# Weight sums by accumulating transfers: moving half of the sums of the plain stages from VectorE to the DMA engines, and one matrix's sums entirely

## The chip, the cores and the metric

The kernel runs on one core of one Trainium2 chip. The metric is the device time of one launch in microseconds (us), the median of three runs. A core has a matrix engine (TensorE, PE in the profile, with its weight loads shown as PEld), a vector engine (VectorE, DVE), a scalar engine (ScalarE, ACT), a general engine (GpSimd, POOL) and an engine that here only issues transfers (SyncE, SP). Transfers between the large memory (DRAM) and the on-chip memory run on 16 DMA engines. A transfer is issued from the SP queue or from the POOL queue; each queue issues in order, and an issue that waits for a semaphore holds up everything behind it on that queue.

## The reference

One inference step of a two-layer decoder on 1024 prompt tokens and 8 decode tokens, all in float32, model width 2048:

```python
def pool_layer(x, prefix, pos, w_in, w_grp, scale, w_out, g_ln, b_ln):
    z = x @ w_in                                   # 2048 -> 4096: u and gate
    u, gate = z[..., :D_POOL], z[..., D_POOL:]
    d, new_state = multiscale_pool(u, prefix, pos) # causal windows 2, 4, 8, 16
    d = jnp.einsum('btgc,gce->btge', d.reshape(B, T, 4, 512), w_grp)
    d = d.reshape(B, T, D_POOL) * scale
    y = (d * jax.nn.silu(gate)) @ w_out
    return layer_norm(ALPHA * x + y, g_ln, b_ln), new_state

def attn_layer(x, pos, kb, vb, ...):               # after kv = h @ w_kv, rotary k
    z = x @ w_in                                   # 2048 -> 4096: q and gate
    o = attn_core(rope(q), kb, vb, ..., sinks)     # window 128, 4 KV heads, 32 heads
    y = (o * jax.nn.silu(gate)) @ w_out
    return layer_norm(ALPHA * x + y, g_ln, b_ln)
```

The outputs are the two results, the new pooling states and the new key and value windows.

## The kernel before

**Stages.** The tokens are cut into two chunks: chunk 0 has 512 prompt tokens, chunk 1 has 512 prompt tokens and the 8 decode tokens. Eight stages follow one another: `ai0`, `ai1` (input product of layer A for chunk 0 and 1, pooling, group product), `ao0`, `ao1` (its output product), `bi0`, `bi1` (key/value, query and gate products of layer B, and the attention), `bo0`, `bo1` (its output product and the last LayerNorm). By the lines that run, `ai0` lasts from 0 to about 410 us, `ai1` to 765, `ao0` and `ao1` to 1110, `bi0` to 1585, `bi1` to about 2030, and the `bo` stages to the end.

**Products.** Every float32 product is made of three fast products: an operand is split into a rounded part ("hi", cast on ACT, line 359) and a remainder ("lo", subtraction on DVE, line 368), and PE multiplies hi by hi, hi by lo and lo by hi. A weight matrix comes in pairs of output tiles; a pair has four blocks of 128 x 1024 numbers (512 KB): a11 and a12 from one tile, a21 and a22 from the other.

- The *plain* stages `ai0` and `bi0` multiply the four blocks as they are (`unit`, lines 529 to 554). One block takes 24 matmuls of 512 columns.
- The other six stages use a seven-product scheme of the Strassen kind (`seven`, lines 439 to 527): three blocks as they are and four sums of blocks. One of the seven takes 24 matmuls of 256 or 260 columns.

**The sums of weights** have to be in DRAM (the tensors `ws`, shown as swia, swoa, swkv, swib, swob in the profile) before a seven-product stage reads them:

- s2 = a21 + a22 (slot 1 of `ws`), s1 = a11 + a21 (slot 2), s3 = a11 + s2 (slot 0), s4 = a12 + s3 (slot 3).
- For `wia`, `wkv` and `wib` they are made beside the plain stage that loads these blocks anyway: `plain_pair` (line 256) puts four calls of `add1` (line 247) on the list `late`, and `end` (line 389) runs one of them per step. `add1` is one addition of 128x1024 on DVE (line 249) and one store issued from POOL (line 250).
- For `woa` and `wob`, which no plain stage reads, `sum_gen` (line 325) does it as side work: 16 parts for each matrix, each with four loads of 256 KB issued from SP (line 334), four additions of 128x512 on DVE (line 342) and four stores of 256 KB issued from POOL (line 343). `woa`'s are put on the side list in `ai0` and must be done before the inputs of `ao0` are begun; ten of `wob`'s parts are put on it in `ai1` and six in `bi0`, and all must be done before the inputs of `bo0` are begun.

**The order of the work** is written out by the program. `begin` (line 380) loads weight blocks five ahead of the one that PE is to multiply (seven, or six, in the seven-product stages), casts four ahead and makes lo three ahead. `end` closes a step: it runs what was put there by `at(n, ...)` ("n steps from now") and, every second or third step, one turn of the first generator on the side list, if enough of the 53 buffers are free. A plain block has two steps of 12 matmuls, a pair therefore eight; one of the seven products is one step of 24 matmuls. Both kinds of step hold about the same PE time. Each engine runs its instructions in the order of the source. In the plain stages POOL also clears small regions that DVE or ACT then fill (line 798 in the pooling, line 1375 in the attention), and in all stages it issues the stores of intermediate results (lines 654, 885, 1014, 1053, 1449).

In `bi1`, after each pair of query tiles, four transfers issued from SP (line 1217) swap partitions; three steps later DVE does the rotary products on what they brought (lines 1225 and 1332), and one step after that PE computes scores from it (line 1360).

## Time and profile before

| quantity | value |
|---|---|
| median of three runs | 2408.71 us (2408.36 to 2408.85) |
| the profiled execution, its own time | 2407.74 us |
| its span, first to last instruction | 2406.0 us |
| DMA queue fed by SP | 482.16 MB, 60.3% of the 16 engines' span |
| DMA queue fed by POOL | 160.88 MB, 16.9% |

The profiled execution was 0.97 us shorter than the median of the runs. A row of grouped instructions gives the line, the engine, the operation, the tile written and the tile read with their shapes, how often it ran, its busy time and the mean of one. A row of a window gives the window, the busy time of each engine with the number of its instructions in brackets, the granted clock of PE (1.00 is full), the mean share of the 16 DMA engines' time that was busy, and the GB/s moved. A DMA's landing time runs from its issue to the last byte. Since matmuls overlap, a busy PE is not proof that it runs at its best rate; the number of matmuls in a window shows that.

### The profile page before, as it was taken

How to read it: one execution, taken by the hardware profiler on the slowest of the kernel's cores; microseconds unless marked ns; L12 is line 12 of the kernel's file. 1: busy time of each engine (PE TensorE's matmuls, PEld its weight loads, DVE VectorE, ACT ScalarE, POOL GpSimd, SP SyncE). 2: the span in 40 equal slices, each digit the busy share in tenths (PEclk: the TensorE clock that was granted, in tenths of full speed). 3: DMA queues.
4: the chain of work that ended last, by engine and by line, in shares of the span. 5: the costliest groups of instructions: out<-in, count | busy, mean ns of one | idle time of the engine just before them, and what ended most of it. 6: DMA issues, size and time to landing. Idle time of an engine off the chain costs nothing.

```text
span 2406.0 us, 43031 instructions
## 1 busy us (share of the span) xinstructions
PE 2368.2 (98%) x16956; PEld 2174.7 (90%) x16956; DVE 1788.4 (74%) x2173; ACT 1244.2 (52%) x2271; POOL 216.2 (9%) x425
## 2 busy tenths in 40 slices
PE   8999999999999999999999999999999999999996
PEld 6888888999999999998878888899999999999996
DVE  8676687767768768867797676786666667788877
ACT  4222224544545546644464445564666667646655
POOL 1121211101010000000011121100000000000000
PEclk9999999999999999999999999999999999999998
DMA  9887888887889879988588766586556558799884
GB/s 387 332 306 271 311 289 290 306 271 263 299 290 313 284 252 326 341 308 293 182 309 296 257 220 213 183 312 206 162 181 196 167 170 292 232 332 366 305 283 140
DMA packets 230875, 645.80 MB, mean 268 GB/s; under 512 B 26256, under 2 KB 74128, under 8 KB 230672
## 3 DMA queue, kind: packets, MB, share of 16 engines
q1 hardware_dynamic: 185328, 482.16, 60.3%
q0 software_dynamic: 45344, 160.88, 16.9%
q8 instruction: 133, 2.18, 0.4%
q14 instruction: 70, 0.57, 0.1%
HBM read 452.07 MB, written 181.36 MB: 263 GB/s over the span
## 4 chain that ended last, share of the span: by engine, by line
PE 54%; DVE 4%; DMA 1%; ACT 1%; issue 1%; SPq 0%; ACTq 0%; DVEq 0%
PE pD L515 11%; PE pD L517 10%; PE pD L516 10%; PE pD L543 5%; PE pD L545 5%; PE pD L544 5%; PE pS L1360 2%; PE pO L1437 2%; PE pS L1413 1%; DVE m L368 1%; PE pO L687 0%; DMA m<-in_woa 0%; DVE m L1147 0%; PE pS L1437 0%; DVE m L1146 0%
## 5 line engine op out<-in xcount | busy, mean ns | idle before, releaser
L515 PE MATMUL pD<-m,m 128*128 128x260 f32 (+1 forms) x3632 | 1031.8, 284 | 5.2 <-DVE m L476 2.9
L517 PE MATMUL pD<-m,m 128*128 128x260 f32 (+1 forms) x3632 | 1024.6, 282 | 1.5 <-DVE m L368 1.4
L516 PE MATMUL pD<-m,m 128*128 128x260 f32 (+1 forms) x3632 | 1024.1, 282 | 0.0
L368 DVE TENSOR_TENSOR m<-m,m 128x1024 fp32r<-128x1024 f32 x614 | 744.1, 1218 | 126.5 <-ACT m L359 99.3
L359 ACT CAST m<-m 128x1024 fp32r<-128x1024 f32 x614 | 637.2, 1048 | 153.0 <-DVE m L368 25.1
L515 PEld LDWEIGHTS pD<-m,m 128*128 128x128 f32 x3632 | 683.7, 188 | 13.9 <-issue 8.2
L517 PEld LDWEIGHTS pD<-m,m 128*128 128x128 f32 x3632 | 684.2, 188 | 2.6 <-DVE m L368 2.3
L516 PEld LDWEIGHTS pD<-m,m 128*128 128x128 f32 x3632 | 683.8, 188 | 1.5 <-issue 1.4
L543 PE MATMUL pD<-m,m 128*128 128x512 f32 x1088 | 432.5, 398 | 7.9 <-ACT m L598 7.9
L544 PE MATMUL pD<-m,m 128*128 128x512 f32 x1088 | 428.4, 394 | 1.2 <-DVE m L607 1.2
L545 PE MATMUL pD<-m,m 128*128 128x512 f32 x1088 | 428.9, 394 | 0.0
L543 PEld LDWEIGHTS pD<-m,m 128*128 128x128 f32 x1088 | 204.7, 188 | 59.1 <-ACT m L598 8.2
L544 PEld LDWEIGHTS pD<-m,m 128*128 128x128 f32 x1088 | 204.8, 188 | 48.6 <-DVE m L607 2.2
L545 PEld LDWEIGHTS pD<-m,m 128*128 128x128 f32 x1088 | 204.5, 188 | 47.7
L249 DVE TENSOR_TENSOR m<-m,m 128x1024 f32<-128x1024 f32 x136 | 166.2, 1222 | 2.8
L488 ACT COPY m<-pD 128x260 f32<-128x260 f32 (+1 forms) x63 | 23.7, 375 | 204.6 <-PE pD L517 204.4
L607 DVE TENSOR_TENSOR m<-m,m 128x1040 fp32r<-128x1040 f32 (+1 forms) x100 | 122.5, 1226 | 6.6 <-ACT m L598 4.4
L598 ACT CAST m<-m 128x1040 fp32r<-128x1040 f32 (+1 forms) x100 | 105.2, 1054 | 13.8 <-DMA m<-in_x 4.1
L1396 ACT ACTIVATE m<-m,sm 128x128 f32<-128x128 f32 x256 | 99.3, 390 | 0.0
L1423 DVE TENSOR_TENSOR m<-pS,cst 128x1024 f32<-128x1024 f32 x32 | 39.2, 1224 | 74.0 <-ACT m L1422 71.5
L863 PE MATMUL pD<-m,m 128*128 128x260 f32 (+1 forms) x528 | 91.4, 323 | 0.0
L481 DVE TENSOR_TENSOR m<-pD,m 128x260 f32<-128x260 f32 (+1 forms) x64 | 27.3, 426 | 85.6 <-PE pD L517 85.5
(190 smaller groups left out, 2058.9 us busy)
## 6 DMA issues: line engine op xcount, KB each, us to landing
m<-in_wia SPq DMA_DIRECT2D x112, 512.0 KB, 6.8
m<-in_wib SPq DMA_DIRECT2D x112, 512.0 KB, 4.7
swia<-m POOLq DMA_DIRECT2D x64, 512.0 KB, 6.8
m<-swia SPq DMA_DIRECT2D x64, 512.0 KB, 6.2
m<-swoa SPq DMA_DIRECT2D x64, 512.0 KB, 5.9
swib<-m POOLq DMA_DIRECT2D x64, 512.0 KB, 5.7
m<-swib SPq DMA_DIRECT2D x64, 512.0 KB, 4.4
m<-swob SPq DMA_DIRECT2D x64, 512.0 KB, 6.1
```

Of the source, the lines that this page charges most:

```text
L249: self.nc.vector.tensor_add(s[out].a[:, :1024], s[a].a[:, :1024], s[b].a[:, :1024])
L359: self.nc.scalar.copy(hi.r[:, :1024], self.stream[self.cast].src().a[:, :1024])
L368: self.nc.vector.tensor_sub(lo.r[:, :1024], s.src().a[:, :1024], hi.a[:, :1024])
L515: nc.tensor.matmul(ps[:, :TH], wh[:, s], h, start=new and k == 0, stop=False, skip_group_check=on)
L516: nc.tensor.matmul(ps[:, :TH], wh[:, s], l, start=False, stop=False, skip_group_check=on)
L517: nc.tensor.matmul(ps[:, :TH], wl[:, s], h, start=False, stop=k == 7, skip_group_check=on)
L543: nc.tensor.matmul(ps[:], wh[:, s], h, start=par == 0 and k == 0, stop=False)
L544: nc.tensor.matmul(ps[:], wh[:, s], l, start=False, stop=False)
L545: nc.tensor.matmul(ps[:], wl[:, s], h, start=False, stop=par == 1 and k == 7)
L598: self.nc.scalar.copy(h.r[:, :n], s.a[:, :n])
L607: self.nc.vector.tensor_sub(l.r[:, :n], s.a[:, :n], h.a[:, :n])
L1396: nc.scalar.activation(x["s3"][:, i, :], x["s3"][:, i, :], AF.Exp, bias=nm[:, i : i + 1], scale=0.125, accum_out=rs[:, i : i + 1],)
```

## The change

1. In the plain stages, two of the four sums of a pair are made by *accumulating transfers*, which POOL issues: when block c (a22) has been split for its product, a21 is read from DRAM once more and added into the buffer of c by the transfer; one step later a11 is added in the same way into the buffer of b (a21). Seven and eight steps after the split of c, the two buffers are stored. The other two sums stay on DVE, at steps eight and nine instead of two and three. The list `late` goes; the six actions are put in place by `at`. Four buffers of a pair are kept six to seven steps longer.
2. `sum_gen("woa")` is divided: parts 0 to 3 in `ai0`, parts 4 to 15 in `ai1`; they must be done when `ao0` starts.
3. `wob`'s sums leave VectorE, and the stages `ai1` and `bi0`. The new `sum_far`, side work in `bi1`, makes them from DRAM to DRAM without a buffer: per pair four plain copies issued from SP and four accumulating transfers issued from POOL, in eight turns; they must be done when `bo0` starts. In `bi1` the side work runs every second step.

```diff
@@ plain_pair
-        late = [
-            self.add1(s, "c", "b", "c", ws[:, 1, :]),
-            self.add1(s, "b", "a", "b", ws[:, 2, :], "b"),
-            self.add1(s, "a", "a", "c", ws[:, 0, :], "c"),
-            self.add1(s, "d", "a", "d", ws[:, 3, :], "a", "d"),
-        ]
+        def more(k, src):
+            return lambda: self.nc.gpsimd.dma_start(s[k].a[:, :1024], src, accum_op=ALU.add)
+        def put(k, i):
+            def go():
+                self.nc.gpsimd.dma_start(ws[:, i, :], s[k].a[:, :1024])
+                if k == "b":
+                    s.pop(k).free(True)
+            return go
+        late = (
+            (0, more("c", a21)), (1, more("b", a11)), (7, put("c", 1)), (8, put("b", 2)),
+            (8, self.add1(s, "a", "a", "c", ws[:, 0, :], "c")),
+            (9, self.add1(s, "d", "a", "d", ws[:, 3, :], "a", "d")),
+        )
...
-            ent("c", a22, [lambda: self.late.extend(late)]),
+            ent("c", a22, [lambda: [self.at(n, go) for n, go in late]]),
@@ new
+    def sum_far(self, name):
+        nc = self.nc
+        add = lambda dst, src: nc.gpsimd.dma_start(dst, src, accum_op=ALU.add)
+        for q in range(8):
+            a, d, b, c = self.quads(name, q)
+            S2, S1, S3, S4 = (self.ws[name][q][:, i, :] for i in range(4))
+            for dst, src in ((S1, b), (S3, a)):
+                nc.sync.dma_start(dst, src)
+            yield
+            for dst, src in ((S2, a), (S4, d)):
+                nc.sync.dma_start(dst, src)
+            yield
+            add(S1, c)
+            yield
+            add(S3, b)
+            yield
+            yield
+            add(S2, S1)
+            yield
+            yield
+            add(S4, S2)
+            yield
@@ end
-        if self.late:
-            self.late.pop(0)()
@@ run
             if (kind, c) == ("ai", 0):
                 add(("x", 1), self.t_gen(("x", 1)))
-                add(("g", 0), self.sum_gen("woa"))
+                add(("g", 0), self.sum_gen("woa", 0, 4))
...
             elif (kind, c) == ("ai", 1):
-                add(("o", 0), self.sum_gen("wob", 0, 10))
+                add("woa", self.sum_gen("woa", 4, 16))
...
+            elif (kind, c) == ("ao", 0):
+                self.ready("woa")
+            elif (kind, c) == ("bi", 1):
+                add("wob", self.sum_far("wob"))
+                self.every, self.room = 2, 0
...
             elif (kind, c) == ("bi", 0):
...
-                add(("o", 0), self.sum_gen("wob", 10, 16))
...
             elif (kind, c) == ("bo", 0):
+                self.ready("wob")
```

(In `sum_far` the names S2, S1, S3, S4 stand for the slots 0, 1, 2, 3 of `ws`.)

2 lines of the change are left out of this document (1 added, 1 removed).

## The prediction

> **What bounds the kernel now.** I read the page's span and busy shares first, then the busy time of each engine by stage, then the number of matmuls in equal windows, and last what PE waited for.
>
> ```profile
> span 2406.0 us, 43031 instructions
> PE 2368.2 (98%) x16956; PEld 2174.7 (90%) x16956; DVE 1788.4 (74%) x2173; ACT 1244.2 (52%) x2271; POOL 216.2 (9%) x425
> ```
>
> ```profile
> core 0: us, PE busy (x) PEld busy (x) DVE busy (x) ACT busy (x) POOL busy (x), PEclk, DMA share, GB/s
> 0.00:25.00 25.00, 15.87 (x59) 11.99 (x60) 15.97 (x15) 15.30 (x15) 0.43 (x6) 1.00 0.95 345
> 25.00:95.00 70.00, 70.00 (x304) 56.82 (x304) 57.23 (x82) 21.27 (x29) 15.38 (x30) 1.00 1.02 402
> 95.00:410.00 315.00, 315.00 (x1363) 255.47 (x1362) 220.11 (x270) 87.78 (x116) 58.15 (x117) 1.00 0.82 286
> 410.00:765.00 355.00, 353.16 (x2935) 352.36 (x2934) 259.99 (x363) 170.59 (x274) 35.28 (x65) 1.00 0.84 290
> 765.00:1110.00 345.00, 344.70 (x2855) 341.07 (x2854) 267.70 (x270) 196.01 (x259) 13.59 (x27) 1.00 0.87 307
> 1110.00:1585.00 475.00, 474.42 (x2549) 383.67 (x2547) 357.23 (x448) 241.25 (x569) 71.83 (x140) 1.00 0.71 245
> 1585.00:2030.00 445.00, 444.29 (x3965) 431.30 (x3964) 300.18 (x365) 288.14 (x662) 9.79 (x18) 1.00 0.63 199
> 2030.00:2380.00 350.00, 345.61 (x2916) 338.25 (x2916) 290.01 (x331) 208.15 (x321) 11.79 (x22) 1.00 0.82 289
> 2380.00:2406.00 26.00, 5.17 (x26) 3.79 (x24) 20.02 (x34) 15.72 (x31) 0.00 (x0) 0.71 0.42 144
> ```
>
> The windows are the stages: `ai0` is the first three, then `ai1`, `ao0` with `ao1`, `bi0`, `bi1`, the `bo` stages, and the end. PE is idle 37.8 us, but 9.1 of these are the start and 20.8 the end, and the change touches neither. In the stages that it touches, PE is idle 1.84 us (`ai1`), 0.30 (`ao`), 0.58 (`bi0`) and 0.71 (`bi1`): 3.4 us together.
>
> A busy PE may still be slow, so the matmuls are counted:
>
> ```profile
> 95.00:155.00 60.00, 60.00 (x261) 1.00 0.84 290
> 155.00:215.00 60.00, 60.00 (x261) 1.00 0.73 262
> 520.00:580.00 60.00, 60.00 (x503) 1.00 0.86 289
> 700.00:760.00 60.00, 58.80 (x490) 1.00 0.83 286
> ```
>
> In `ai0` 261 matmuls of 512 columns start in 60 us, 0.230 us each, whether the DMA engines are 84% or 73% busy. In `ai1` it is 503 of 260 columns (0.119 us), or 490 where the window shows 1.2 us idle; 13 x 0.119 = 1.55 us agrees. So there is no hidden slowness for the change to win. The Trainium skill says in "Trainium Kernel Development and Optimization" (Performance Expectations) that matmul busy time is a bad metric for the distance to the best, because matmuls are pipelined; by that rule the 98% bounds no gain, and the trace agrees that it alone would not, but the counts do.
>
> What PE waited for, by the list of waits for `ai1`, for `bi0` and for `bi1`:
>
> ```profile
> PE pD L515 <- DVE m L476: 1.8, 3, 1.0
> PE pS L1360 <- DVE m L1332: 0.6, 2, 0.4
> PE pD L515 <- ACT pD L456: 0.7, 1, 0.7
> ```
>
> **Part 1: two of four sums per pair in the plain stages.** There are 34 pairs (16 of `wia`, 2 of `wkv`, 16 of `wib`), four additions each.
>
> ```profile
> L249 DVE TENSOR_TENSOR m<-m,m 128x1024 f32<-128x1024 f32 x136 | 166.2, 1222 | 2.8
> DMA to landing us min/median/max: 5.6/8.2/11.4
> DMA to landing us min/median/max: 2.9/6.1/8.4
> ```
>
> (The landing rows are those of the stores of line 250 from 20 to 100 us and from 100 to 410 us.) DVE loses 68 x 1.222 = 83 us. I count this as a gain of 0.3 us: in `ai0` after the start PE waits for nothing, and in `bi0` for DVE only 0.6 us. Added are 68 accumulating transfers of 512 KB; the stores stay 136.
>
> The trace has no accumulating transfer. It cannot land sooner than a store does (6.1 us), since it moves the same bytes; and if it reads its destination too, two stores' time is the nearest row: 12.2 us, or 16.4 in the crowded first 100 us. Now the deadline. A pair takes eight steps of 12 matmuls, 8 x 12 x 0.230 = 22.1 us. On POOL the order is: accumulate into c, one step (2.8 us) later into b, stores of both at steps 7 and 8, then the next pair's accumulate. POOL's stores wait for the landing, and so does DVE at step 8 (a + c). The cycle holds as long as landing + 2.8 + about 1 us for the wait on DVE and the issues stays under 22.1, that is up to about 18.3 us. Both 12.2 and 16.4 are under it. I take 12 us, the upper end, because an addition needs the old value, and a cost of nothing. The cover is lo made ahead, and it is thick, as one place shows:
>
> ```profile
> 79.41 0.69 DVE L342 TENSOR_TENSOR m<-m 128x512 f32<-128x512 f32 x1 [8.20 <-DMA m<-in_woa]
> 0.00:79.30 79.30, 18.12 (x15) 1.00 1.00 391
> 0.00:79.30 79.30, 70.17 (x294) 1.00 1.00 391
> ```
>
> DVE stood still 8.2 us for a late load and PE did not stop. At its end DVE had made 15 lo's (second row, line 368) and PE had done 294 matmuls, 12.25 blocks of 24: 2.75 blocks, 15 us, were left. A wait of DVE under some 15 us is free if it does not come again with every pair. If that cover is gone, each further us is a us of time. What is queued behind a waiting POOL: the clearing of line 798 (line 1375 in `bi0`), for which DVE waits next, and the stores of lines 885 and 654, nothing of which is used soon.
>
> Traffic, by the window from 25 to 95 us, where 402 GB/s was all that the DMA engines gave (share 1.02): the 32 transfers in `ai0` are 16.8 MB (42 us of DMA time), twice that if each reads twice. The skill states the second ("Collectives: The Full Stack", "The bandwidth ceiling: the fold count and why AG ≠ RS ≠ AR": an add in the DMA path needs two source reads and ran at about half the rate). By single reads the cost of this part is 0, and by the skill's rule too, with a landing of 12 us. No run here shows which holds.
>
> Buffers: four per pair for six to seven steps longer out of eight are three more of 53. The part of `sum_gen` that goes frees its four. Cost nothing; if the cover is gone, side work is put off, which has room in `bi0`.
>
> **Part 2: `woa` later, `wob` out of `ai1` and `bi0`.** The additions of `sum_gen` by stage (`ai0`, `ai1`, `ao`, `bi0`):
>
> ```profile
> 0.00:410.00 410.00, 32.15 (x47) 1.00 0.86 310
> 410.00:765.00 355.00, 34.89 (x51) 1.00 0.84 290
> 765.00:1110.00 345.00, 4.10 (x6) 1.00 0.87 307
> 1110.00:1585.00 475.00, 16.21 (x24) 1.00 0.71 245
> ```
>
> After it, `ai0` has 16 and `ai1` 48, the others none. Each addition goes with a 256 KB load on SP and a 256 KB store on POOL, 0.52 MB together. `ai0` loses 31 of each (21 us of DVE, 16 MB: the weight of the 16.8 MB added); `bi0` loses 24 (13 MB) and gains 36 transfers (19 MB, at most 38), so 25 MB / 402 GB/s = 63 us of 475 at most, from share 0.71 to 0.84. No stage fills up for long. `ai1` keeps 48 of 51 additions; its 1.84 us of idle PE is for line 476, subtractions queued on DVE behind pooling and sums. Gain 0.3 us (0 to 1.8). Twelve parts at four turns are 48 turns of the 60 that 120 steps give, so `ao0` finds them done.
>
> **Part 3: `sum_far` in `bi1`.** 32 copies of 512 KB on SP (16.8 MB) and 32 accumulating ones on POOL (16.8 to 33.6 MB): 84 to 125 us of DMA time in 445 us, from share 0.63 to 0.82 or 0.91. No engine computes for it. POOL carries only 18 stores there, so its waits harm little. SP is what matters, as the partition swaps share its queue:
>
> ```profile
> 1699.84 2.41 SPq L1217 DMA_DIRECT2D m<-m  x4
> DMA to landing us min/median/max: 2.6/5.2/6.7
> 1711.48 2.38 DVE L1225 TENSOR_TENSOR m<-m,m 128x1040 f32<-128x1040 f32 x2
> 1713.90 1.24 DVE L1332 TENSOR_TENSOR m<-m,m 128x1040 f32<-128x1040 f32 x1
> 1716.55 1.93 PE pS L1360 x16
> ```
>
> The last swap is issued at 1702.2 and lands 5.2 us later (second row, all swaps of `bi1`), 4 us before DVE wants it; the rotary work ends at 1715.1 and PE uses it at 1716.55. A swap up to 4 + 1.4 us late is free here. Two copies just ahead of it are 1.05 MB, 2.6 us. In eight pairs of query tiles this may cost 0 to 4 us; I take 0.5.
>
> Turns: `bi1` has 126 steps, 63 turns; the last 14 steps are barred, as 14 input pieces are then outstanding and twice as many buffers would have to be free. So about 56 turns are run, seven of the eight pairs; the eighth is issued in one go at the start of `bo0`, between its weight and input loads:
>
> ```profile
> 2030.00:2060.00 30.00, 30.00 (x266) 28.77 (x266) 27.38 (x30) 28.56 (x64) 0.54 (x1) 1.00 0.82 281
> 2060.00:2090.00 30.00, 29.52 (x284) 27.60 (x283) 19.27 (x31) 15.90 (x34) 0.54 (x1) 1.00 0.65 211
> ```
>
> There ACT is busy 28.6 of 30 us and DVE 27.4: little cover. Four copies (2.1 MB, 5.2 us of DMA) stand ahead of loads on SP's queue. I take 1.5 us, between 0 and 8 (5.2 us of copies and half as much again of accumulates).
>
> **Sum**, against the profiled execution's 2407.74 us: -0.3 (`bi0`) -0.3 (`ai1`) +0.5 (`bi1`) +1.5 (`bo0`) = +1.4, so 2409.1; that execution stands 0.97 us under the median, so the median becomes 2410.1 us. A measurement of this kernel tells 0.2% (4.8 us) from no change.
>
> **Rivals.**
>
> - *Accumulates too slow (slower).* Place: POOL's queue in `ai0`, at the stores at steps 7 and 8. Point: a landing over 18.3 us. From there each of the 16 pairs of `ai0` lasts that much longer, less 15 us of cover once: with 22 us, 16 x 3.7 - 15 = 44 us, so about 2453; `bi0`'s 18 pairs have 475 / 18 = 26 us each, so they follow only later. For it: the first 100 us have stores up to 11.4 us, and twice that is over the point. Against: for the rest of `ai0` it would need three times the 6.1 us. Chance 0.14.
> - *SP and the DMA engines crowd `bi1` and the start of `bo0` (slower).* All the upper bounds above: 4 + 8 = 12 us, so about 2421. For it: ACT and DVE are nearly full at 2030. Against: `bi1` has share 0.63. Chance 0.18.
> - *The relief of DVE pays (faster).* DVE loses 83 + 44 us of additions (64 of line 342 at 0.68 us for `wob`). If all idle PE in the touched stages went, 3.4 us: 2405.3, still within 0.2%. Over 0.2% would need the gaps of the `bo` stages too (4.4 us from 2030 to 2380), which the change does not touch: 2401. Chance 0.06 for that.
>
> **How the numbers follow.** The forecast, within 0.2% (2403.9 to 2413.5), has 0.62; slower is 0.14 + 0.18 = 0.32; faster 0.06. The time is 2410. The likeliest case alone reaches from 2405 (all idle gone) to 2413.5. The range, 2404.5 to 2425, takes in the crowded boundary with some room, and leaves out the slow accumulates and the large gain, 0.2 together.
>
> **What would show it.** Right: 68 additions on line 249, 261 matmuls per 60 us in `ai0` as before, landings of the accumulating transfers under 18 us, PE idle in `ai0` and `bi0` unchanged. Line 342 gone after 765 us. Wrong: windows of `ai0` with fewer than 261 matmuls and DVE or POOL waiting there for the accumulating transfers; line 1360 waiting for line 1332 in `bi1`; PE idle at 2030 to 2060 behind ACT's casts.

## The result, and the profile after

The changed kernel takes 2538.89 us (median of four runs, 2536.07 to 2540.22) where the kernel before took 2408.72 us beside it: 1.0539 times as long, with a 95% interval of 1.0521 to 1.0557. The forecast was 2410.1 us and no change. It was wrong by 129 us, and the time lies far outside the range.

The page of the changed kernel, its span, its busy shares, and the slices for the granted clock and for the DMA engines:

```profile
span 2538.4 us, 42849 instructions
PE 2400.9 (95%) x16956; PEld 2192.9 (86%) x16956; DVE 1670.6 (66%) x2041; ACT 1245.0 (49%) x2271; POOL 269.1 (11%) x461
...
PEclk9977799999999999999999999999999999999998
DMA  9999999998888877998969777878655556799884
```

The span grew by 132.4 us. PE is idle 137.5 us in place of 37.8, which is 99.7 us of it. The other 32.7 us are busy time: the same 16956 matmuls took 2400.9 us in place of 2368.2. The clock row says where: three slices of 63 us near the start have a granted clock of 7 tenths.

The same execution in windows of 60 us in `ai0`, then by stage (`bi0`, `bi1`, the `bo` stages; columns as in the prediction's windows):

```profile
60.00:120.00 60.00, 53.81 (x217) 42.23 (x216) 20.48 (x27) 10.60 (x12) 13.80 (x22) 0.94 1.03 328
120.00:180.00 60.00, 34.82 (x130) 25.71 (x128) 15.79 (x22) 6.24 (x9) 11.34 (x16) 0.81 1.03 275
180.00:240.00 60.00, 29.43 (x96) 22.35 (x97) 18.99 (x26) 6.40 (x10) 13.45 (x23) 0.71 1.02 288
240.00:300.00 60.00, 34.34 (x107) 25.00 (x106) 15.39 (x18) 9.52 (x13) 14.27 (x21) 0.75 1.02 274
300.00:360.00 60.00, 59.25 (x253) 47.29 (x253) 25.06 (x32) 12.78 (x17) 17.83 (x28) 0.99 1.02 288
...
1226.00:1701.00 475.00, 467.12 (x2483) 377.94 (x2482) 288.31 (x376) 234.90 (x554) 87.44 (x145) 0.99 0.82 244
1701.00:2164.00 463.00, 456.09 (x4031) 441.21 (x4030) 311.06 (x378) 295.26 (x676) 12.73 (x24) 0.99 0.64 205
2164.00:2517.00 353.00, 347.72 (x2921) 339.99 (x2920) 293.05 (x335) 209.91 (x325) 11.76 (x22) 1.00 0.83 287
```

Before, each of these windows of `ai0` had 261 matmuls. Now it is 217, 130, 96 and 107, with the DMA engines busy all the time; from 120 to 300 us PE is busy about half of the time, at a clock of 0.71 to 0.81. `bi1` has a DMA share of 0.64. The prediction had expected 0.82 to 0.91 there, from `sum_far`. So `sum_far` did not run in `bi1`.

The trace by source line says where it ran: the four lines of `sum_far` that issue transfers (370 and 373 on SP, 365 on POOL), with the times of the first and last issue, and the time from issue to landing of line 370's copies:

```profile
L370 SPq DMA_DIRECT2D swob<-in_wob x16: 490/496/634, 45.4 to 238.6; - x16
L373 SPq DMA_DIRECT2D swob<-in_wob x16: 490/496/645, 78.3 to 246.7; - x16
L365 POOL DMA_DIRECT2D swob<-in_wob x16: 802/838/1087, 67.1 to 321.4; - x16
L365 POOL DMA_DIRECT2D swob<-swob x16: 802/850/881, 99.8 to 340.0; - x16
...
DMA to landing us min/median/max: 13.8/23.8/38.6
```

All 64 transfers of `sum_far` were issued between 45 and 340 us, in `ai0`, five stages ahead of the place at which the source makes them. They depend on nothing but inputs and each other. The sentence above that each engine runs its instructions in the order of the source holds only for PE, DVE and ACT, which the program ties to it (`in_order`). On SP and POOL the order comes out of the build of the program, and here transfers that wait for nothing stand near the front.

What this did to `ai0` is in the list of waits of the changed kernel from 45 to 345 us (what waited, for what, us in total, how often, the longest):

```profile
ACT m L395 <- DMA m<-in_wia: 186.9, 15, 50.0
DVE m L404 <- ACT m L395: 66.7, 10, 14.9
...
PE pD L579 <- DVE m L404: 48.5, 8, 29.2
...
PE pD L577 <- ACT m L395: 33.1, 6, 8.9
```

ACT's cast is the first consumer of a loaded weight block, and it waits 187 us for loads; DVE's subtraction waits for the cast, and PE for both. The loads are late for more than one reason. They share 16 full DMA engines with `sum_far`. This is the landing time of the loads on line 243 from 45 to 345 us, in the kernel before and then in the changed one:

```profile
DMA to landing us min/median/max: 3.7/6.8/13.8
```

```profile
DMA to landing us min/median/max: 6.7/14.2/38.3
```

The other reason is POOL's queue. This is the trace around PE's longest wait, the 29.2 us that end at 199.9 us (start, duration, line, what; the bracket is what ended the idle time ahead of it):

```profile
195.58 0.13 POOL L832 MEMSET m<- 128x15 f32 x1
195.74 1.42 DVE L843 TENSOR_TENSOR m<-m 128x514 f32<-128x514 f32 x2 [35.93 <-POOL m L832]
198.61 1.22 DVE L404 TENSOR_TENSOR m<-m,m 128x1024 fp32r<-128x1024 f32 x1
```

DVE stands 35.9 us for a region that POOL clears, and the subtraction that PE needs is behind that on DVE. In these 36 us POOL issues six of `sum_far`'s accumulates and stands some 15 us for landings between them. Stores that free buffers come late on POOL as well: SP stands 32.8 us for one of `tg`, and issues no load from 177 to 210 us. The prediction had named this clearing as what is queued behind a waiting POOL. How the loss divides between the full engines and POOL's order is not shown; e4 below bears on it.

The clock belongs to the same story. The Trainium skill ("TensorE: Matmul & The Clock Gate", "HAM oscillation — how this bites in real kernels") says that waits for DMA long enough to leave the array idle for a window put the clock back, so that what follows starts slowly. The trace agrees: PE waits of up to 29.2 us, and a granted clock of 0.71 where it was 1.00.

To see where each kernel of the study loses, I compared when the same matmul (the n-th in PE's order, which is the same in all) starts in it and in the kernel before. The table gives the lag that is added in each stretch of the kernel before, in us. It is worked out from the traces, so it is that of the profiled execution, which can stand some us off the median (e4's is 6.4 us above it, e8b's 4.4 below); the first column is the median time of the whole kernel. The column of `ai0` takes in the turn to `ai1`.

```
                        time us  25-432  432-766  766-1112  1112-1578  1578-1614  1614-2031  2031-2083
                                 (ai0)   (ai1)    (ao)      (bi0)      (to bi1)   (bi1)      (bo0 start)
after                   2538.89  117.0   -2.8     -0.4       9.5        9.0        0.3        0.0
e1_pairs_only           2433.84   11.7   -1.0     -0.4      13.2        2.4        0.1        0.0
e2_far_only             2500.39   97.6   -2.6     -0.1      -0.3       -0.1        0.0        0.0
e3_pinned               2434.24    0.0   -2.8     -0.4       9.0        6.6        5.2        9.5
e4_adds_pinned          2473.76   43.8   -2.8     -0.3      10.2        6.1       14.1        1.4
e5_far_pinned_only      2431.92   -0.6   -2.6      0.8      -0.3        4.8       14.8        6.4
e8b_far_small           2432.17    6.1   -2.6     -0.2      -0.3        3.3       10.8        3.6
e6_half_far             2406.02   -0.6   -2.6     -0.2       0.1        0.0        1.0        0.0
e10_half_far_step0      2408.60   -0.6   -2.6     -0.1       0.2        0.0        3.5        0.0
e7_half_far_acc_ai0     2405.76    0.1   -2.8     -0.4      -1.3        0.5        1.2        0.1
e11_dve_only            2406.65    0.0   -0.9     -0.2      -0.2        0.0        0.3        0.0
e9_early_puts           2455.96    7.3   -2.6      0.5      12.6       12.2       15.1        7.0
e12_late_puts1          2436.70    0.5   -2.5      0.1      12.0        7.9        1.8       10.8
e13_puts_pinned         2431.62    1.3   -2.8     -0.4       5.5        5.5        5.4        9.0
e14_half_far_acc        2428.53    0.0   -2.8      0.1      18.8        2.8        0.7        0.0
e15_half_far_acc_pinned 2417.02    0.7   -2.8     -0.3       6.2        2.5        0.9        0.0
e16_pairs_puts_pinned   2433.31    9.1   -1.0     -0.3      14.0        5.4        0.1        0.0
e17_copies_for_adds     2418.81    1.1   -1.0     -0.1       5.8        5.6        0.1        0.0
e18_adds_late           2421.61    3.8   -1.0     -0.3       5.5        6.0        0.2        0.0
```

Of the 132 us of the change, 117 are lost in `ai0` and 18.5 in `bi0` and at the turn to `bi1`.

### The profile page after: what moved, and what is told of

It is laid out like the page before. It is cut to its first block, busy times and chain, and to the rows that moved or that the text cites. A ratio compares the mean times of both kernels' runs of the same rounds, so it can differ in the third digit from the quotient of the medians.

```text
span 2538.4 us, 42849 instructions
## 1 busy us (share of the span) xinstructions
PE 2400.9 (95%) x16956; PEld 2192.9 (86%) x16956; DVE 1670.6 (66%) x2041; ACT 1245.0 (49%) x2271; POOL 269.1 (11%) x461
## 5 line engine op out<-in xcount | busy, mean ns | idle before, releaser
L579 PE MATMUL pD<-m,m 128*128 128x512 f32 x1088 | 438.1, 403 | 49.2 <-DVE m L404 49.0
L577 PE MATMUL pD<-m,m 128*128 128x512 f32 x1088 | 440.4, 405 | 41.3 <-ACT m L395 33.4
L578 PE MATMUL pD<-m,m 128*128 128x512 f32 x1088 | 435.5, 400 | 0.5 <-DVE m L641 0.5
L249 DVE TENSOR_TENSOR m<-m,m 128x1024 f32<-128x1024 f32 x68 | 83.0, 1220 | 52.2 <-DMA m<-in_wia 51.7
L843 DVE TENSOR_TENSOR m<-m 128x512 f32<-128x512 f32 (+5 forms) x80 | 55.8, 697 | 84.5 <-POOL m L832 48.7
```

What stands on the lines that cost most here:

```text
L577: nc.tensor.matmul(ps[:], wh[:, s], h, start=par == 0 and k == 0, stop=False)
L578: nc.tensor.matmul(ps[:], wh[:, s], l, start=False, stop=False)
L579: nc.tensor.matmul(ps[:], wl[:, s], h, start=False, stop=par == 1 and k == 7)
```

## The experiments

### First: is it the place of `sum_far`?

My theory (Q in the expectations) was that the early `sum_far` is the loss. The rival (P) was the prediction's own first rival: the plain pairs' accumulating transfers, too slow on POOL.

**e1_pairs_only**: part 1 alone. `woa` and `wob` are summed by `sum_gen` in the stages of the kernel before.

```diff
-                add(("g", 0), self.sum_gen("woa", 0, 4))
+                add(("g", 0), self.sum_gen("woa"))
-                add("woa", self.sum_gen("woa", 4, 16))
+                add(("o", 0), self.sum_gen("wob", 0, 10))
-                add("wob", self.sum_far("wob"))
+                (in bi0)  add(("o", 0), self.sum_gen("wob", 10, 16))
```

> Only part 1 (two of four sums per pair in the plain stages by accumulating transfers); the sums of woa and wob as before. Theory Q (the 64 transfers of sum_far, which wait for nothing, ran at 45 to 340 us in stage ai0 instead of in bi1, and starved it): 2403 to 2418 us, 261 matmuls per 60 us in ai0 after the start. Rival P (the accumulating transfers of the plain pairs themselves are too slow): 2480 us or more, with ai0 as thin as in the changed kernel.

Measured: 2433.84 us, 1.0103 times before (1.0088 to 1.0118).

**e2_far_only**: parts 2 and 3 alone. `plain_pair` is that of the kernel before.

```diff
-            (0, more("c", a21)), (1, more("b", a11)), (7, put("c", 1)), (8, put("b", 2)),
+            self.add1(s, "c", "b", "c", ws[:, 1, :]),
+            self.add1(s, "b", "a", "b", ws[:, 2, :], "b"),
...
```

> Only parts 2 and 3 (woa divided, wob by sum_far); the plain pairs as before. Theory Q: 2490 to 2540 us, most of the loss. Rival P: 2405 to 2420 us.

Measured: 2500.39 us, 1.0382 (1.0365 to 1.0400).

**e3_pinned**: the whole change, but each transfer of `sum_far` is tied to the instruction that stands ahead of it in the source on its queue. This is an order and no wait. (The edit is shortened here.)

```diff
+def in_order(tc, pins):
+    for i in instructions:
+        if i.name in pins and i.engine in prev:
+            tc.add_manual_dep(i, prev[i.engine].name, NoSync)
+        prev[i.engine] = i
...
-                nc.sync.dma_start(dst, src)
+                self.pinned(lambda: nc.sync.dma_start(dst, src))
-        add = lambda dst, src: nc.gpsimd.dma_start(dst, src, accum_op=ALU.add)
+        add = lambda dst, src: self.pinned(lambda: nc.gpsimd.dma_start(dst, src, accum_op=ALU.add))
```

> The whole change, but each of sum_far's transfers keeps its place of the source behind the transfer before it on its queue, so that they run in bi1. Theory Q: 2404 to 2425 us, ai0 full again, some loss in bi1 and at the start of bo0 possible. Rival P: 2480 us or more, as nothing changes for the plain pairs.

Measured: 2434.24 us, 1.0108 (1.0093 to 1.0123).

**e4_adds_pinned**: as e3, but only POOL's 32 accumulating transfers are tied; SP's 32 copies go early.

```diff
-                self.pinned(lambda: nc.sync.dma_start(dst, src))
+                nc.sync.dma_start(dst, src)
```

> As the last, but only the 32 accumulating transfers of sum_far (POOL) keep their place in bi1; the 32 copies (SP) are free to run early. If it is the bytes on the DMA engines and the places on SP's queue that starve ai0: 2450 to 2500 us. If it is POOL, waiting in its queue for one sum_far step after the other while the clearing of line 832 and the accumulates of the pairs stand behind: 2404 to 2425 us.

Measured: 2473.76 us, 1.0275 (1.0258 to 1.0291).

What follows: holding 64 transfers in place, and changing nothing else, takes the time from 2538.89 to 2434.24 us. 104.7 of the 130.2 us are the place of `sum_far`, and `ai0` is back to a lag of 0. Parts 2 and 3 alone, let go early, lose 97.6 us in `ai0` with no accumulating transfer of a plain pair there. The early copies alone (e4) lose 43.8 us there, inside what was expected if bytes and places on SP's queue do it. The rest of `ai0`'s loss needs the early accumulates, and with them goes DVE's wait for POOL's clearing: 48.7 us from 60 to 300 us in the changed kernel, 25.3 in e2, 3.6 in e4 and in e3.

Theory Q missed on e1 and e3: it gave the plain pairs and the held `sum_far` nothing (up to 2418 and 2425 us), and both kernels are 25 us slower than before. That rest is the subject of all that follows.

### The bytes or the places in the queues?

**e5_far_pinned_only**: e2, with `sum_far` held in place as in e3.

```diff
-        add = lambda dst, src: nc.gpsimd.dma_start(dst, src, accum_op=ALU.add)
+        add = lambda dst, src: self.pinned(lambda: nc.gpsimd.dma_start(dst, src, accum_op=ALU.add))
-                nc.sync.dma_start(dst, src)
+                self.pinned(lambda: nc.sync.dma_start(dst, src))
```

> Parts 2 and 3 alone, with sum_far's transfers held at their place in bi1, and the plain pairs on VectorE as before. Beside it stand the plain pairs alone (2433.84 us, 25 over before) and the whole change held in place (2434.24 us, 26 over). Theory S, the parts of the pinned kernel are separate: by its lag against before, matmul by matmul, some 15 us came in bi0 from the plain pairs, -3 in ai1 from the divided woa, 4.5 in bi1 and 10 at the start of bo0 from sum_far. Without the pairs the time is 2416 to 2424 us, bi0 shows no new wait of PE, and the loss is all after 1600 us. Rival P, the plain pairs carry all of it, and the lag in bi1 and bo0 came from their late start: the time is 2404 to 2411 us.

Measured: 2431.92 us (2428.3 to 2437.2), 1.0101 (1.0087 to 1.0115). Both theories miss. Part 1 alone costs 25 us, parts 2 and 3 in place cost 23, and all together 26. The table shows the two ways in which they do not add. Part 1 alone loses 11.7 us at the end of `ai0`, where all of `woa` is still summed; with part 2, e3 loses none there. And `sum_far` loses 19.6 us at the turn to `bi1` and in it when it is alone, but 5.2 in `bi1` behind the plain pairs' loss. The second half of this I can't explain: the same transfers at the same steps meet other loads.

The first is plain from two windows of `ai0`, e1's and then e3's:

```profile
95.00:410.00 315.00, 315.00 (x1363) 255.67 (x1363) 188.05 (x240) 86.03 (x113) 82.94 (x147) 1.00 1.01 335
```

```profile
95.00:410.00 315.00, 315.00 (x1363) 255.51 (x1362) 176.79 (x219) 90.39 (x119) 67.11 (x118) 1.00 0.91 291
```

With `woa`'s sums and the accumulates in one stage the DMA engines are full (1.01), and the first operands of `ai1` come late: all 11.7 us are lost around 420 us. With 12 of the 16 parts moved the share is 0.91, and nothing is lost there.

**e8b_far_small**: e5, with each transfer of `sum_far` divided. Columns 0 to 127 go in a transfer that is free to go early, the other 896 columns in one that is held in `bi1`.

```diff
+        def go(eng, dst, src, **k):
+            eng.dma_start(dst[:, :128], src[:, :128], **k)
+            self.pinned(lambda: eng.dma_start(dst[:, 128:], src[:, 128:], **k))
```

> The same as the kernel with only parts 2 and 3 held in place, but each of sum_far's 64 transfers is divided: its first 128 of 1024 columns go in a transfer that is free to go early, the other 896 columns in one held in bi1. So as many transfers as before are early in ai0 in SP's and POOL's queues, with an eighth of the bytes. Theory B, the bytes: ai0 loses an eighth of the 98 us that it lost when all were early, some 12 us, and the time is 8 to 20 us over that of the kernel held in place. Rival N, the places: SP and POOL spend as long on issuing as before and PE's operands come behind them, so ai0 loses most of the 98 us: the time is 50 to 100 us over that of the kernel held in place.

Measured: 2432.17 us, 1.0103 (1.0088 to 1.0119), 0.3 us over e5. As many transfers as in e2 stood early in both queues, and `ai0` lost 6.1 us, not 97.6. Theory N falls: the number of places in the queues is not the price. Theory B misses as well: its 12 us in `ai0` was twice what it cost, and its 8 to 20 us over e5 did not come. By the table the later stages gave the 6 us back, but the profiled execution of e8b was 4.4 us under its median, so that is not certain. So the early transfers hurt by something that shrinks with their bytes. That is the DMA time, and also the waits for landings in POOL's queue, which shrink with it (from 60 to 300 us DVE waits 6.1 us for POOL's clearing here, 25.3 in e2); this run doesn't part the two.

### How much of `sum_far` does a stage bear?

**e6_half_far**: plain pairs as before, `woa` divided, `wob`'s pairs 0 to 3 by `sum_gen` in `bi0`, and pairs 4 to 7 by `sum_far`, held in place, from step 20 of `bi1`.

```diff
+                (in bi0)  add("wob", self.sum_gen("wob", 0, 8))
-                add("wob", self.sum_far("wob"))
+                self.at(20, lambda: add("wob", self.sum_far("wob", 4, 8)))
```

> Half of part 3, held in place: wob's pairs 0 to 3 are summed on VectorE in bi0, pairs 4 to 7 by sum_far from step 20 of bi1 on; woa divided as in part 2; plain pairs as before. If sum_far's price is set by how many of its transfers stand beside bo0's early loads and bi1's (10 and 4.5 us for eight pairs), half of them cost 3 to 7 us, the divided woa gives 3 back, and the time is 2406 to 2413 us. If the price is a threshold that four pairs do not pass, it is 2403 to 2407 us, faster than before. If VectorE's sums in bi0 now make PE wait there, it is over 2413 us.

Measured: 2406.02 us, 0.9992 (0.9983 to 1.0001).

**e10_half_far_step0**: the same, begun at the first step of `bi1`.

```diff
-                self.at(20, lambda: add("wob", self.sum_far("wob", 4, 8)))
+                add("wob", self.sum_far("wob", 4, 8))
```

> The kernel with half of part 3 (2406.02 us), with its four pairs of sum_far begun at the first step of bi1 in place of step 20. With eight pairs from the first step (2431.92 us) 13 us were lost in the first 70 us of bi1, 5 at 1885 us and 7.5 at the start of bo0. Theory E, the entry into the stage: sum_far's transfers meet the loads with which bi1 starts (DMA busy 0.91 to 0.97 there). The four pairs lose the same 13 us: 2416 to 2423 us. Rival M, the number of pairs: four in a stage of 450 us are no load: 2403 to 2409 us.

Measured: 2408.60 us, 1.0002 (0.9993 to 1.0011).

**e7_half_far_acc_ai0**: e6, with part 1's accumulating pairs for `wia` in `ai0` alone.

```diff
+        if name != "wia":
+            late = (the four additions on VectorE, at steps 0 to 3)
```

> As the kernel with half of part 3, and the plain pairs of wia (ai0) by accumulating transfers, those of bi0 on VectorE as before. Theory A, accumulates cost nothing in ai0 (the whole change held in place had no lag there) and their price in bi0 is that stage's: the time is within 4 us of the kernel with half of part 3 alone. Rival L, ai0 has no room either: the plain pairs alone lost 11.7 us at the change from ai0 to ai1, where DMA was busy 1.01 of the time all through ai0, and here the time is 8 to 15 us longer than with half of part 3 alone.

Measured: 2405.76 us, 0.9990 (0.9982 to 0.9999).

**e11_dve_only**: no sum by a transfer at all. `woa` is divided at part 10, `wob`'s parts 0 to 8 are in `ai1` and 8 to 16 in `bi0`.

```diff
-                add(("g", 0), self.sum_gen("woa", 0, 4))
+                add(("g", 0), self.sum_gen("woa", 0, 10))
-                add("woa", self.sum_gen("woa", 4, 16))
+                add("woa", self.sum_gen("woa", 10, 16))
+                add("wob", self.sum_gen("wob", 0, 8))
...
+                (in bi0)  add("wob", self.sum_gen("wob", 8, 16))
```

> Part 2 alone, with no sums by transfers: woa's parts 0 to 10 in ai0 and 10 to 16 in ai1, wob's parts 0 to 8 in ai1 and 8 to 16 in bi0, all on VectorE. The kernels with half of part 3 were 2.4 to 2.7 us faster than before, and by their lag all of it came in ai1 (1 us at 655, 1.2 at 749 us). If it is the dividing of woa that gives it, and the transfers nothing, this kernel is 2404 to 2407 us. If VectorE's relief in bi0 and bi1 was part of it, it is 2408 us or more, since ai1 has more additions here than before (56 for 40).

Measured: 2406.65 us, 0.9993 (0.9985 to 1.0002).

What follows. Four pairs of `sum_far` in `bi1` cost 1 us from step 20 and 3.5 from the first step; eight pairs cost 26. Theory E's range is missed, and rival M holds for the most part: it is the number of pairs. Whether the price grows step by step or past a threshold stays open, as e6 lies in both of its ranges. The entry into the stage has its share, as the eight pairs show. These are windows of the kernel before, of e5 and of e6 at the start of `bi1`:

```profile
1590.00:1630.00 40.00, 40.00 (x351) 39.69 (x350) 31.22 (x34) 30.84 (x59) 0.56 (x1) 1.00 0.74 256
```

```profile
1590.00:1630.00 40.00, 35.44 (x297) 34.90 (x296) 25.76 (x29) 26.20 (x54) 3.16 (x4) 0.91 0.91 301
```

```profile
1590.00:1630.00 40.00, 40.00 (x367) 39.48 (x365) 30.18 (x33) 30.24 (x59) 0.55 (x1) 1.00 0.74 259
```

And these are e5's timeline there (start, duration, line, what; x2 is two in a row) and its waits from 1600 to 1700 us:

```profile
1594.32 3.15 SPq L375 DMA_DIRECT2D swob<-in_wob  x2
1597.57 1.10 SPq L251 DMA_DIRECT2D m<-swkv  x2
```

```profile
1612.84 1.04 ACT L397 CAST m<-m 128x1024 fp32r<-128x1024 f32 x1 [5.20 <-DMA m<-swkv]
1613.79 1.00 ACT L1460 COPY m<-pS 128x1024 f32<-128x1024 f32 x1
```

```profile
PE pS L1398 <- DVE m L1370: 5.3, 1, 5.3
...
PE pS L1475 <- DVE m L1461: 4.6, 1, 4.6
...
DVE m L1263 <- DMA m<-m: 4.0, 1, 4.0
```

SP issues two copies of `sum_far` at 1594.32, and two loads of `swkv` behind them. ACT waits 5.2 us for such a load, ACT's next instruction is the copy (line 1460) that DVE's line 1461 needs, and PE waits 4.6 us for that. This is a stall through ACT's order, which the prediction did not have. The larger wait is the one that it did have: lines 1398 and 1370 here are 1360 and 1332 of the kernel before, PE behind the rotary products. SP issues two copies of `sum_far` at 1652.14 us and the four partition swaps at 1659.35; the swaps land after 13.3 to 13.6 us, where the median of the kernel before was 5.2. DVE waits 4.0 us for them (line 1263) and PE 5.3 us, until 1678.6.

The small gain of e6 and e7 is in `ai1`. Theory A holds for `ai0`: accumulates there cost nothing once `woa` is divided (e7 against e6). These are the fastest kernels of the study, about 0.1% faster than before. That is less than a measurement of this kernel can tell, and VectorE alone (e11) comes within a microsecond of them, although its 0.9 us in `ai1` is no gain of its own: e1, whose `ai1` is that of the kernel before, has 1.0 too.

### Why the plain pairs cost time in `bi0`

**e9_early_puts** and **e12_late_puts1**: e3, with the stores of `c` and `b` and the two additions moved.

```diff
-            (7, put("c", 1)), (8, put("b", 2)), (8, a + c), (9, a + d)
+ e9         (4, put("c", 1)), (5, put("b", 2)), (5, a + c), (6, a + d)
+ e12        (8, put("c", 1)), (9, put("b", 2)), (9, a + c), (10, a + d)
```

> The whole change held in place (2434.24 us), with the plain pairs' stores of c and b at steps 4 and 5 in place of 7 and 8, and the two additions at 5 and 6 in place of 8 and 9. It is about the 14.6 us that this kernel loses in bi0 (at 1260 us and at 1600 us). Theory W, POOL's waits: in bi0 POOL stands 59.8 us of one 170 us stretch at the stores for the landing of the accumulates, and the next accumulate, the stores of th and the stores that free buffers stand behind. Earlier stores wait longer: these waits grow and the time is 2437 to 2460 us. Theory H, the buffers: the pair's four buffers are held six to seven steps longer than without the accumulates. Three steps less give back a half: below 2428 us.

> The opposite of the kernel with early stores: the whole change held in place, with the stores of c and b at steps 8 and 9 and the additions at 9 and 10, one step (some 3 us) later. Theory W: POOL waits less at them (some 30 us in place of 59.8 in the same stretch), and the 14.6 us in bi0 shrink to under 9: below 2428 us. Theory H: the buffers are held longer, and the time is 2437 us or more.

Measured: e9 2455.96 us, 1.0198 (1.0184 to 1.0212); e12 2436.70 us, 1.0114 (1.0098 to 1.0129). Earlier stores cost 22 us more, a time that W expected and the opposite of H; but by the table only 3.6 us of it are lost in `bi0`, and where the rest comes from was not taken apart. Later stores should have helped by W, and they cost 2.5 us, which H just misses. POOL's wait at the stores of `swib` for the landing, from 1110 to 1600 us, is 198.4 us in e3, 218.2 with earlier and 209.9 with later stores; W expected later stores to halve it in the stretch that it looked at. So the step in the source was not what set POOL's wait, and the timeline says why. This is POOL in the kernel e14 (below), where part 1 stands in both stages and the stores are where the build puts them. Line 273 is the accumulating transfer, line 277 the store of `c` or `b`, and the bracket is what ended POOL's idle time ahead of it:

```profile
1224.50 0.86 POOL L273 DMA_DIRECT2D m<-in_wib  x1 [0.95 <-PE pS L1460]
1228.60 0.55 POOL L277 DMA_DIRECT2D swib<-m  x1 [3.23 <-DMA m<-in_wib]
1236.76 0.53 POOL L277 DMA_DIRECT2D swib<-m  x1 [7.61 <-DVE m L697]
1237.28 0.33 POOL L1422 MEMSET m<- 128x256 f32 x1
1237.53 0.53 POOL L701 DMA_DIRECT2D th<-m  x1
1238.17 0.91 POOL L273 DMA_DIRECT2D m<-in_wib  x1
...
1241.17 0.88 POOL L273 DMA_DIRECT2D m<-in_wib  x1 [1.00 <-DVE m L1428]
1247.77 0.55 POOL L277 DMA_DIRECT2D swib<-m  x1 [5.71 <-DMA m<-in_wib]
1255.33 0.53 POOL L277 DMA_DIRECT2D swib<-m  x1 [7.01 <-DMA m<-in_wib]
```

The source has six steps, some 17 us, between an accumulate and the store of its buffer. In POOL's queue the two stores of a pair stand right behind its two accumulates. POOL stands 3 to 8 us at each of the four stores shown, mostly until the landing, and the stores that free buffers, the clearing of line 1422 and the next accumulates all come late. It is the same cause as `sum_far`'s, in small: POOL's order isn't the source's.

**e13_puts_pinned**: e3, with these stores tied to their place in POOL's queue.

```diff
-                self.nc.gpsimd.dma_start(ws[:, i, :], s[k].a[:, :1024])
+                self.pinned(lambda: self.nc.gpsimd.dma_start(ws[:, i, :], s[k].a[:, :1024]))
```

> The whole change with sum_far's transfers held in place (2434.24 us), and now also the plain pairs' stores of c and b held at their place in POOL's queue, at steps 7 and 8. In the trace of the kernel without this, POOL issues the store right behind its accumulate (accumulates at 1236.57 and 1239.42, stores at 1245.44 and 1252.98 us), although the source has six steps, some 17 us, between them, so that POOL stands until each landing. Theory O, this order is what bi0 loses by: POOL's waits for the landing shrink to a few us and the 14.6 us of bi0 go: 2416 to 2424 us. Rival D, the DMA time of the accumulates (2.2 times that of a store for each byte): the order changes nothing, 2430 us or more.

Measured: 2431.62 us, 1.0097 (1.0082 to 1.0112).

**e14_half_far_acc**: e6 with part 1 whole (in e7's code, without its `if`). **e15_half_far_acc_pinned**: the same with e13's edit.

> The kernel with half of part 3, and part 1 in both ai0 and bi0, with the stores where the build puts them. Its neighbour with the accumulates in ai0 alone took 2405.76 us. The accumulates of bi0 then cost by themselves what the lag of the whole change showed there, some 14 us: 2415 to 2424 us by theories O and D alike. If it is under 2410, bi0's loss came from their meeting with sum_far's eight pairs.

> As the one before, with the plain pairs' stores of c and b held at steps 7 and 8 in POOL's queue. Theory O: 2404 to 2409 us, as fast as with the accumulates in ai0 alone. Rival D: as the one before, 2415 us or more.

Measured: e14 2428.53 us, 1.0079 (1.0064 to 1.0094); e15 2417.02 us, 1.0038 (1.0026 to 1.0050).

**e16_pairs_puts_pinned**: e1 with e13's edit.

> Part 1 alone (2433.84 us) with the plain pairs' stores of c and b held at steps 7 and 8. Part 1 alone lost 11.7 us at the end of ai0, where all of woa's sums are made beside the accumulates and DMA was busy 1.01 of the time, and 15 in bi0. Theory O for bi0 and DMA time for ai0: only the 15 go, 2416 to 2424 us. If the order was the cause in ai0 too: 2406 to 2414 us. Rival D for both: 2430 us or more.

Measured: 2433.31 us, 1.0097 (1.0081 to 1.0114).

By the ranges, rival D is right in e13, e15 and e16 and theory O in none; e14 is over the range that both gave. The traces say more: the order is a part of it. Between e14 and e15, where nothing else is in the way, the stores in place give 11.5 us back, all of it in `bi0`. POOL's waits for the landing, from 1110 to 1600 us, in e14 and then, by the list of who waited for the accumulates, in e15:

```profile
POOL swib L277 <- DMA m<-in_wib: 188.1, 30, 10.8
```

```profile
POOL swkv L277: 19.7, 2
POOL swib L277: 1.8, 2
DMA to landing us min/median/max: 5.8/8.9/12.5
```

POOL's 188 us of waiting at the stores of `swib` fall to 1.8 (two stores of `swkv` still wait 19.7), at the same landing (5.6/8.6/13.8 us in e14). In e13 the edit gives 4.6 us back in `bi0` and at its end, of 15.6. In e16 it gives nothing. So order was not all of it, and e15 is still 8.6 us slower than before.

### What the rest is

**e17_copies_for_adds**: e16, with plain loads in place of the accumulating transfers. `c` and `b` are overwritten, so the sums `S1` to `S4` of the plain pairs are left out and other values stand in their place. Number, bytes, queue, order and buffers stay; POOL's issue gets shorter too, 0.53 us in the median in place of 0.89.

```diff
-            self.nc.gpsimd.dma_start(s[k].a[:, :1024], src, accum_op=ALU.add)
+            self.nc.gpsimd.dma_start(s[k].a[:, :1024], src)
```

> Part 1 alone with the stores held in place (2433.31 us), but the 68 accumulating transfers are plain loads of the same bytes into the same buffers: they overwrite c and b instead of adding to them, so the sums S1 to S4 of the plain pairs are left out of the result and other values take their place. Number, bytes, queue, order and buffers stay; only the adding goes. Theory A, the accumulate's price on the DMA engines (2.2 times a store's time per byte, some 110 us of all 16 engines beyond a plain load) is what still costs 24 us: 2406 to 2416 us. Rival H, the buffers held and the places in the queues: 2425 us or more.

Measured: 2418.81 us, 1.0043 (1.0027 to 1.0060).

**e18_adds_late**: e1 without any accumulating transfer. VectorE makes all four sums, at the steps of the change.

```diff
-            (0, more("c", a21)), (1, more("b", a11)), (7, put("c", 1)), (8, put("b", 2)),
+            (7, self.add1(s, "c", "b", "c", ws[:, 1, :])),
+            (8, self.add1(s, "b", "a", "b", ws[:, 2, :], "b")),
```

> Part 1 alone without any accumulating transfer: VectorE makes all four sums of a plain pair as before, but at steps 7, 8, 8 and 9 in place of 0 to 3, so the four buffers of a pair are held as long as in the change. Rival H, the buffers: most of the 25 us of part 1 stay, 2420 us or more. Theory A: 2406 to 2412 us; a few us more than before where the buffers add to it.

Measured: 2421.61 us, 1.0057 (1.0042 to 1.0072).

By the ranges, e17 lies between theory A and rival H, and e18 is in H's. Each theory has half. Against the kernel before on the same chip, e16 is 24.9 us slower and e17 11.1. Taking away the adding alone (its DMA time and its longer issue) thus gives 13.8 us back, by the lags 8 of the 9.1 in `ai0` and 8.2 of the 14.0 in `bi0`. Keeping only the held buffers, with all four additions on VectorE as before but late, costs 13.9 us: 3.8 in `ai0` and 11.5 in `bi0` and at its end. The e17 rest (11.4 us in `bi0` and at its end) is the same size and in the same stretches as e18's. I read it as the buffers, since late additions of all four sums are in e18 alone and the hold is in both; what a longer hold does to SP's loads was not taken apart further.

The DMA time of the adding is in the page's rows for the queue of POOL's transfers (packets, MB, share of 16 engines' span), for the kernel before, e16 and e17:

```profile
q0 software_dynamic: 45344, 160.88, 16.9%
```

```profile
q0 software_dynamic: 55136, 196.54, 24.5%
```

```profile
q0 software_dynamic: 55136, 196.54, 21.3%
```

In us of all 16 engines: 0.169 x 2406.0 = 406.6, 0.245 x 2432.5 = 596.0, 0.213 x 2417.2 = 514.9. If the queue's other transfers need the same time in all three, the 35.66 MB added take 189.4 us with adding (188 GB/s) and 108.3 without (329 GB/s). So the adding costs 1.75 times a plain load.

## Why the prediction was wrong

**The step that failed is Part 3's place: "`sum_far` in `bi1`".** The working took the source's order for SP's and POOL's, counted 63 turns in `bi1`, and priced the copies against swaps and casts there. None of the 64 transfers was there. Out of their place they cost 104.7 us (after against e3), by the table in `ai0`, a stage that the change's diff doesn't name for them. The profile of before could have told. This is a row of line 243 there, the loads of `wob`'s sums for the `bo` stages, first and last issue:

```profile
L243 SPq DMA_DIRECT2D m<-swob x64: 319/326/4881, 1848.8 to 2336.1; - x64
```

`bo0` begins at 2030 us, and the first of these loads was issued at 1848.8 us, some 50 steps ahead (126 steps take 445 us), where the source loads at most seven blocks ahead. So at least one load had gone ahead of its place, as far as a free buffer let it, as I read it. I didn't read the row, and it alone would not have said how far a transfer goes that needs no buffer at all.

**Part 1's deadline stood on the same error.** "On POOL the order is: accumulate into c, one step later into b, stores of both at steps 7 and 8" was not POOL's order, so the bound of 18.3 us for the landing was never in force. The landing itself was within what I took, 12 us: 5.6/8.6/13.8 in `bi0` (e14). Its price of nothing was wrong. Alone, part 1 costs 25 us: 13.8 for the adding (e16 against e17) and 13.9 for the longer hold of the buffers, as I read e18, which together are a little more than the whole. I had both causes in the working and set both to nothing, the traffic since 84% of a stage is not full, and the buffers since three more of 53 seemed few. The order of the stores, which I did not have, costs 11.5 us where it can be seen alone (e14 against e15).

**The rate of the adding.** The measured rate for an accumulate is 188 GB/s and that of the plain load in its place 329, which is 0.57 of it; with either rate the working had put the cost at nothing. The Trainium skill ("Collectives: The Full Stack", "The bandwidth ceiling: the fold count and why AG ≠ RS ≠ AR") has a rate of about half, and for that it gives two source reads. The trace agrees with the rate; that two reads are the cause, no run here shows.

**Part 2** was right in sign: -2.8 us in `ai1`, against a forecast of -0.3 with a bound of -1.8. 1.0 of it is also in e1, whose `ai1` has the sums of the kernel before, so it isn't the change's; the rest is the bound. What I missed is that the moved sums also make room in `ai0` (1.01 to 0.91), without which the accumulates cost 11.7 us there.

**Part 3's prices in place** were mis-sized too. Held in `bi1`, `sum_far` costs 19.6 us at the turn and in `bi1` (I took 0.5, bound 4) and 6.4 at the start of `bo0` (I took 1.5, bound 8), by e5. The second is inside the bound, the first far out of it. Its larger single wait, 5.3 us, is the one that the working had listed, line 1360 for line 1332 behind the swaps: two copies ahead of them were to make them 2.6 us late, and they landed some 8 us later than the median before. The other, 4.6 us, is ACT behind a load of `swkv`, which the working did not have.

**The rivals.** "Accumulates too slow" named the right stage and the wrong transfer: the plain pairs' landings stayed under its point (16.6 us at most in the changed kernel), and with `sum_far` out of `ai0` (e1, e3) that stage keeps its 1363 matmuls from 95 to 410 us. "SP and the DMA engines crowd `bi1` and the start of `bo0`" is what happens when the change does what its source says (e5 and e3), with the sign that it named, at twice its price. None of the cases had the early transfers, so no bound of the range came near.

**What stands of the first part:** PE was the bound, DVE's relief paid next to nothing (118 us less of DVE's busy time, and `ai1` alone faster, by 2 us), and the counts of matmuls told the loss at once.

## What to carry to other kernels

Before you price a moved transfer, find out who sets the order of the queue that issues it: here SP's and POOL's queues were not in the order of the source, and 64 transfers that waited for nothing but each other went five stages ahead, at 105 us. The place at which a similar transfer starts in the trace of before, against its place in the source, is the row to look for. And a sum that VectorE made beside a bound PE cost next to nothing here (e11 is 0.1% from the kernel before), while the same sum in a transfer costs 1.75 loads' worth of DMA time and its buffers a longer hold. I'd expect it to pay only in a stage where the compute engine is the bound and the DMA engines aren't; no run here shows such a stage.

## What the runs showed of the hardware

- An accumulating transfer of 512 KB from DRAM into SBUF takes the DMA engines 1.75 times as long as a plain load of the same bytes on the same queue (188 and 329 GB/s over all 16), but lands hardly later: 5.5/9.2/14.4 us (e16) against 4.1/8.1/14.7 (e17), from issue to landing over 95 to 1600 us.
- POOL's issue of one takes 0.89 us in the median (e16), where a plain load of the same bytes in its place takes 0.53 (e17).
- Copies of 512 KB from DRAM to DRAM landed after 23.8 us in the median and 38.6 at most while the engines were full (line 370's 16 in the changed kernel's `ai0`).
- A starved PE lost twice: 99.7 us of idle time, and 32.7 us of longer busy time for the same matmuls, with a granted clock down to 0.71 in windows of 60 us.
